# The two FFN down products and the mixer's output product: seven block products in place of eight

## The chip, the cores and the metric

One core of one Trainium2 chip. The metric is the time of one execution on the device, in microseconds (us), as the median of several runs; lower is better.

## What is computed

A decoder trunk on x of 512 tokens by 1024 features: one layer with a short convolution mixer, one with forgetting attention, an FFN behind each. The attention part is not touched by the change. The three products that are changed are `@ w_out` of the mixer and `@ w_down` of the two FFNs:

```python
def short_conv_mixer(xn, w_in, conv_w, w_out):
    proj = xn @ w_in
    b, c, h = jnp.split(proj, 3, axis=-1)
    u = causal_dwconv(c * h, conv_w)
    return (b * u) @ w_out            # 1024 x 1024

def conv_ffn(xn, w_up, conv_w, w_down):
    up = xn @ w_up
    a, g = jnp.split(up, 2, axis=-1)
    a = causal_dwconv(a, conv_w)
    return (jax.nn.silu(a) * g) @ w_down   # 2816 x 1024
...
x = x + short_conv_mixer(rmsnorm(x), ...)
x = x + conv_ffn(rmsnorm(x), ...)
```

## The kernel before

Features lie on the 128 partitions and tokens along the free dimension, so x is eight tiles of 128x512 (k-tiles). Every product is done in fp32r pieces: `split` and `parts` cut an fp32 tile into `hi` (a rounding copy on ACT) and `lo` (source minus hi, on DVE), and `mac` issues hi·hi, hi·lo and lo·hi for each half of 256 tokens: six matmuls of 128x256 for one k-tile and one output tile. Weights come by DMA as 128x1024 tiles (`wraw`, 3 buffers) on SP's queue, and are split 512 columns at a time (`whi`, `wlo`, 4 buffers each), shortly before they are used.

The stages follow each other: the mixer (24 products of eight k-tiles, then the output product `a_out`), FFN0, attention, its output product, FFN1. An FFN makes 22 hidden tiles; tile j needs two up products (`pa`, `pg`) of 48 matmuls each. `pa` is scaled (L316, DVE), convolved (L241 on ACT, L242 and L244 on DVE) and put through silu (L192, ACT); `pg` is scaled (L322, DVE) and multiplied by that on POOL (L323), and the result is split (L162 on ACT, L163 on DVE). When all 22 stand, `project` makes the eight output tiles one after the other, each over 22 k-tiles (132 matmuls), and adds the old x on the way out of PSUM (L271, DVE). `Norm.add` then splits the new x with the next norm's gain (L168, L169) and adds its squares up on POOL (L224).

The order on each engine is what the Tile scheduler makes of the program. PSUM has eight banks of 128x512; `mmps` hands out six of them in turn. One pool `big` of 58 tiles of 128x512 serves all stages.

Of the kernel before, what the change touches and what calls it, by code (L numbers as in the profile page):

```python
# [53 lines left out]
def trunk(ctx: ExitStack, tc: tile.TileContext, x_t, a_in, a_out, up0, down0, wk, wv, wf, wqg, b_out,  # L54
# [40 lines left out]
    x = [G() for _ in range(KT)]  # L95
# [10 lines left out]
    def parts(raw, n):  # L106

        hi = new(wsp, "whi", [P, T], F32R)
        lo = new(wsp, "wlo", [P, T], F32R)
        nc.scalar.copy(out=hi[:, :n], in_=raw)  # L110
        nc.vector.tensor_tensor(out=lo[:, :n], in0=raw, in1=hi[:, :n].bitcast(F32), op=ALU.subtract)  # L111
        return [(hi[:, c:c + P], lo[:, c:c + P]) for c in range(0, n, P)]

    def weights(src, nk=KT):

        cuts = [0, 8] if nk == 8 else [0, 8, 15, 22]
        for c0, c1 in zip(cuts[:-1], cuts[1:]):
            raw = new(wraw, "wraw", [P, 1024], F32)
            nc.sync.dma_start(out=raw[:, :(c1 - c0) * P], in_=src[:, c0 * P:c1 * P])
            for c in range(0, c1 - c0, 4):  # L120
                n = min(4, c1 - c0 - c) * P
                yield from parts(raw[:, c * P:c * P + n], n)
# [18 lines left out]
    def gemm2(srcs, xs, hold=1):

        pss, kept = [], []
        for src in srcs:
            ps = mmps()
            late = []
            for k, w in enumerate(weights(src)):
                if k < KT - hold:
                    mac(ps, w, xs[k], k == 0, False)
                else:  # L150
                    late.append((k, w))
            pss.append(ps)
            kept.append(late)
        for ps, late in zip(pss, kept):
            for k, w in late:
                mac(ps, w, xs[k], False, k == KT - 1)
# [9 lines left out]
    def scaled_split(src, gain):  # L166
        hi, lo = G(F32R), G(F32R)
# [36 lines left out]
    class Norm:  # L204
# [21 lines left out]

        def finish(self):
            ps = bank("at")
            hi, lo = split(self.acc, M(F32R), M(F32R))
# [18 lines left out]
    def back(m):  # L248
        t = new(misc, "ld", [P, T], F32, bufs=3)
        nc.sync.dma_start(out=t, in_=xsp[m])  # L250
        return t

    def project(src, hs, nk, norm, last=False, spilled=False, spill=False, pss=()):

        for m in range(KT):
            if m < len(pss):
                ps = pss[m]
            elif nk == KT and m < 2:
                if m == 0:
                    pss = gemm2((src[0], src[1]), hs)  # L260
                ps = pss[m]
# [68 lines left out]
    def attention(norm, nxt_norm):  # L330
# [426 lines left out]
        for k in range(KT):  # L757
            x[k] = None
# [120 lines left out]
```

## Time and profile before

| | before |
|---|---|
| median of 3 runs | 1234.31 us (1233.61 to 1234.62) |
| the profiled execution | 1233.1 us |
| its span, first to last instruction | 1231.3 us |
| busy: PE / DVE / ACT / POOL | 1216.5 / 678.6 / 537.4 / 203.1 us |
| mean granted TensorE clock | 0.996 of full speed |

The span is the stretch that the trace covers; the profiled execution's own time is 1.8 us longer. Busy times of different engines overlap, so they are to be compared with the span one by one.

### The profile page before, as it was taken

To read this page: it belongs to the slowest core of one execution; us is meant where nothing else is said; L and a number is where in the kernel's file an instruction comes from. 1 tells how busy PE (TensorE), PEld (TensorE's weight loads), DVE (VectorE), ACT (ScalarE), POOL (GpSimd) and SP (SyncE) were. 2 spreads that over 40 slices of the span, in tenths; PEclk is the share of its full clock that TensorE was granted. 3 is DMA by queue.
4 is the path that set the end of the run, shared out by engine and by line. 5 is a ranking of instruction groups with operands and counts; after the bars stand their busy time and mean duration, and the time that the engine had idled before them with its cause. 6 is when DMAs were issued, how large, how long until landed. Compare 5 with 4: busy or idle time off the path is not lost.

```text
span 1231.3 us, 24568 instructions
## 1 busy us (share of the span) xinstructions
PE 1216.5 (99%) x10425; PEld 1189.0 (97%) x10425; DVE 678.6 (55%) x1163; ACT 537.4 (44%) x973; POOL 203.1 (16%) x181
## 2 busy tenths in 40 slices
PE   9999999999999999999999899999999999999998
PEld 8999999999999999999998788889999999999998
DVE  6755556555555533344646787876565555553222
ACT  5433345334333433333556767775543334342221
POOL 0100021111111100000123435442111111110000
PEclk9999999999999999999999999999999999999999
DMA  6233233333333344342342212124233233233341
GB/s 215 87 103 101 88 104 92 97 104 93 97 104 91 93 130 125 121 140 87 95 139 79 84 52 86 53 87 129 86 104 101 89 103 101 89 99 104 116 119 45
DMA packets 39374, 124.14 MB, mean 101 GB/s; under 512 B 4384, under 2 KB 4896, under 8 KB 39264
## 3 DMA queue, kind: packets, MB, share of 16 engines
q1 hardware_dynamic: 38048, 120.41, 31.8%
q10 hardware_dynamic: 1152, 1.97, 0.5%
q8 instruction: 81, 1.33, 0.4%
q14 instruction: 29, 0.24, 0.1%
q0 software_dynamic: 64, 0.20, 0.0%
HBM read 118.33 MB, written 4.23 MB: 100 GB/s over the span
## 4 chain that ended last, share of the span: by engine, by line
PE 90%; ACT 4%; DVE 3%; POOL 2%; issue 1%; DMA 0%; SPq 0%; DVEq 0%; POOLq 0%; ACTq 0%
PE st L131 18%; PE st L130 17%; PE st L132 17%; PE mm L130 11%; PE mm L132 11%; PE mm L131 11%; ACT s L189 1%; PE st L620 1%; PE at L658 1%; PE st L649 1%; POOL m L667 1%; DVE s L624 1%; DVE wlo L111 1%; ACT g L189 1%; ACT g L162 1%
## 5 line engine op out<-in xcount | busy, mean ns | idle before, releaser
L130 PE MATMUL st<-g,whi 128*128 128x256 f32 x1686 | 465.5, 276 | 0.0
L131 PE MATMUL st<-g,whi 128*128 128x256 f32 x1686 | 465.4, 276 | 0.0
L132 PE MATMUL st<-g,wlo 128*128 128x256 f32 x1686 | 465.4, 276 | 0.0
L110 ACT CAST whi<-wraw 128x512 fp32r<-128x512 f32 (+1 forms) x394 | 240.4, 611 | 473.6 <-PE st L131 291.9
L111 DVE TENSOR_TENSOR wlo<-wraw,whi 128x512 fp32r<-128x512 f32 (+1 forms) x394 | 283.6, 720 | 222.9 <-ACT whi L110 218.3
L130 PE MATMUL mm<-g,whi 128*128 128x256 f32 x1242 | 346.2, 279 | 0.0
L131 PE MATMUL mm<-g,whi 128*128 128x256 f32 x1242 | 343.5, 277 | 0.0
L132 PE MATMUL mm<-g,wlo 128*128 128x256 f32 x1242 | 343.5, 277 | 0.0
L130 PEld LDWEIGHTS st<-g,whi 128*128 128x128 f32 x1686 | 316.6, 188 | 0.1
L131 PEld LDWEIGHTS st<-g,whi 128*128 128x128 f32 x1686 | 316.5, 188 | 0.1
L132 PEld LDWEIGHTS st<-g,wlo 128*128 128x128 f32 x1686 | 316.5, 188 | 0.0
L130 PEld LDWEIGHTS mm<-g,whi 128*128 128x128 f32 x1242 | 233.5, 188 | 1.8
L131 PEld LDWEIGHTS mm<-g,whi 128*128 128x128 f32 x1242 | 233.4, 188 | 1.3
L132 PEld LDWEIGHTS mm<-g,wlo 128*128 128x128 f32 x1242 | 233.2, 188 | 0.1
L323 POOL TENSOR_TENSOR m<-m,m 128x512 f32<-128x512 f32 x44 | 69.1, 1573 | 408.3 <-DVE m L322 370.9
L162 ACT CAST g<-m 128x512 fp32r<-128x512 f32 x66 | 40.8, 619 | 90.4 <-POOL m L323 66.8
L163 DVE TENSOR_TENSOR g<-m,g 128x512 fp32r<-128x512 f32 x51 | 36.8, 722 | 67.3 <-ACT g L162 66.7
L224 POOL TENSOR_TENSOR m<-m,m 128x512 f32<-128x512 f32 x21 | 27.9, 1330 | 175.5 <-ACT m L222 153.6
L640 POOL TENSOR_SCALAR s<-s,sm 128x128 f32<-128x128 f32 (+3 forms) x64 | 41.4, 660 | 75.5 <-DVE sm L637 69.2
L189 ACT ACTIVATE s<-s,bb 128x128 f32<-128x128 f32 (+3 forms) x64 | 35.4, 555 | 22.9 <-DVE bb L633 22.8
L241 ACT ACTIVATE m<-m,pr 128x512 f32<-128x512 f32 x52 | 37.7, 725 | 15.9 <-DVE m L316 13.0
L242 DVE SCALAR_TENSOR_TENSOR m<-m,pr,m 128x511 f32<-128x511 f32 x52 | 39.0, 750 | 9.5 <-ACT m L241 9.5
(170 smaller groups left out, 1312.3 us busy)
## 6 DMA issues: line engine op xcount, KB each, us to landing
wraw<-up SPq DMA_DIRECT2D x88, 512.0 KB, 3.5
wraw<-down SPq DMA_DIRECT2D x32, 448.0 KB, 3.5
wraw<-a_in SPq DMA_DIRECT2D x21, 512.0 KB, 3.6
wraw<-down SPq DMA_DIRECT2D x16, 512.0 KB, 3.5
wraw<-wqg SPq DMA_DIRECT2D x16, 512.0 KB, 3.6
wraw<-a_out SPq DMA_DIRECT2D x8, 512.0 KB, 3.5
ld<-xsp SPq DMA_DIRECT2D x16, 256.0 KB, 2.8
wraw<-wv SPq DMA_DIRECT2D x8, 512.0 KB, 3.6
```

Of the source, the lines that this page charges most:

```text
L110: nc.scalar.copy(out=hi[:, :n], in_=raw)
L111: nc.vector.tensor_tensor(out=lo[:, :n], in0=raw, in1=hi[:, :n].bitcast(F32), op=ALU.subtract)
L130: nc.tensor.matmul(ps[:, f], lhsT=lh[0], rhs=rh[0][:, f], start=go, stop=False, skip_group_check=True)
L131: nc.tensor.matmul(ps[:, f], lhsT=lh[0], rhs=rh[1][:, f], start=False, stop=False, skip_group_check=True)
L132: nc.tensor.matmul(ps[:, f], lhsT=lh[1], rhs=rh[0][:, f], start=False, stop=end, skip_group_check=True)
L162: nc.scalar.copy(out=hi, in_=src)
L163: (eng or nc.vector).tensor_tensor(out=lo, in0=src, in1=hi.bitcast(F32), op=ALU.subtract)
L189: chain["exp"] = ordered(nc.scalar.activation(**kw), chain["set"])
L241: nc.scalar.activation(out=y, in_=src, func=AF.Copy, scale=pr[:, col + 2:col + 3])
L242: nc.vector.scalar_tensor_tensor(out=y[:, 1:T], in0=src[:, 0:T - 1], scalar=pr[:, col + 1:col + 2], in1=y[:, 1:T], op0=ALU.mult, op1=ALU.add)
L323: nc.gpsimd.tensor_tensor(out=g, in0=g, in1=y, op=ALU.mult)
L640: nc.gpsimd.tensor_scalar(out=s, in0=s, scalar1=sm[:, e:e + 1], scalar2=1.0, op0=ALU.mult, op1=ALU.mult)
```

## The change

A pair of k-tiles by the two halves of the tokens is a 2x2 arrangement of 128x256 blocks (`f`, a tile of 128x1024), and a pair of output tiles by a pair of k-tiles is a 2x2 arrangement of weight blocks. `Seven` makes the products of such arrangements with seven block products, numbered 1 to 7, in place of eight. For it, `operands` makes the sums and differences of the activation blocks (DVE), and `add_up` those of the weight blocks (POOL: three adds, of 2b, b and b columns, where b is 128 times the number n of pairs of k-tiles in the call). The seven results are put together from two PSUM banks, through copies of a bank on ACT (`early`), sums on DVE and POOL (`sums`, `run`) and `end` on DVE.

The down products are no longer made in one go: `ffn_line` puts a part of them behind hidden tile 6 (n = 3), behind tile 14 (n = 4) and behind tile 21 (n = 4), and x goes through DRAM (`xsp`) between the parts. The last part of each FFN and the mixer's output product are called with `hold`: there the first two `Seven`s run all pairs but the last before the last one is ready. The product of pg and silu on POOL (`late`, L661 after the change) is put into the program one hidden tile later.

Tiles come from pools of each stage. `Line` prepares weights ahead in an order of its own (12 tiles of 128x1024, `w`), in steps that `step`, `mid` and `use` set. `in_order` pins ACT, DVE and POOL to the order of the program in the mixer and in both FFNs. Weights are rearranged on the host so that a `Seven` reads its four blocks side by side.

```diff
-    big = ctx.enter_context(tc.tile_pool(name="big", bufs=58))
-    sp = ctx.enter_context(tc.tile_pool(name="sp", bufs=10))
-    ptp = ctx.enter_context(tc.tile_pool(name="ptp", bufs=6))
     misc = ctx.enter_context(tc.tile_pool(name="misc", bufs=8))
     small = ctx.enter_context(tc.tile_pool(name="small", bufs=3))
-    wraw = ctx.enter_context(tc.tile_pool(name="wraw", bufs=3))
-    wsp = ctx.enter_context(tc.tile_pool(name="wsp", bufs=4))
+    normed_ = ctx.enter_context(tc.tile_pool(name="norm", bufs=16))
+    raws_ = ctx.enter_context(tc.tile_pool(name="raw", bufs=4))
...
+    def in_order(*engines):
...
+    def operands(f, between=None):
+        t, v = S(), blocks(f)
+        tv = blocks(t)
+        nc.vector.tensor_tensor(out=tv[:, 0:2], in0=v[:, 0:4:3], in1=v[:, 1:2].to_broadcast([P, 2, HT]),
+                                op=ALU.subtract)
+        for out, in0, in1 in ((2, tv[:, 1], v[:, 0]), (3, tv[:, 2], v[:, 2])):
+            nc.vector.scalar_tensor_tensor(out=tv[:, out], in0=in0, scalar=-1.0, in1=in1, op0=ALU.mult, op1=ALU.subtract)
+        ops = {}
+        for names, src in (("13", v[:, 0:4:3]), ("57", tv[:, 0:2]), ("64", tv[:, 2:4])):
+            hi, lo = G(F32R), GL(F32R)
+            nc.scalar.copy(out=blocks(hi), in_=src)
+            nc.vector.tensor_tensor(out=blocks(lo), in0=src, in1=blocks(hi).bitcast(F32), op=ALU.subtract)
+            for h, n in enumerate(names):
+                ops[n] = hi[:, h * HT:(h + 1) * HT], lo[:, h * HT:(h + 1) * HT]
+            if between is not None and names == "57":
+                between()
+        g = G(F32R)
+        nc.scalar.copy(out=g[:, 0:HT], in_=v[:, 2])
+        nc.vector.tensor_tensor(out=g[:, HT:T], in0=v[:, 2], in1=g[:, 0:HT].bitcast(F32), op=ALU.subtract)
+        ops["2"] = g[:, 0:HT], g[:, HT:T]
+        return ops
...
+    class Seven:
+        size, raws = 7, 2
+        def __init__(self, src, n):
+            self.n, self.src = n, src
+            self.b = n * P
+        def load(self):
+            b = self.b
+            self.raw = R(), R()
+            for h, r in enumerate(self.raw):
+                nc.sync.dma_start(out=r[:, 0:2 * b], in_=self.src[:, 2 * h * b:2 * (h + 1) * b])
+        done = None
+        def add_up(self):
+            if self.done is None:
+                b, (r0, r1) = self.b, self.raw
+                s, s2 = self.done = S(), S()
+                nc.gpsimd.tensor_tensor(out=blocks(s[:, 0:2 * b], b), in0=blocks(r0[:, 0:2 * b], b),
+                                        in1=blocks(r1[:, b:2 * b], b).to_broadcast([P, 2, b]), op=ALU.add)
+                nc.gpsimd.tensor_tensor(out=s2[:, 0:b], in0=s[:, 0:b], in1=r0[:, b:2 * b], op=ALU.add)
+                nc.gpsimd.tensor_tensor(out=s2[:, b:2 * b], in0=s2[:, 0:b], in1=r1[:, 0:b], op=ALU.add)
+        def prepare(self):
+            self.add_up()
+            b, (r0, r1), (s, s2) = self.b, self.raw, self.done
...
+            for names, raw in (("14", r0), ("75", s), ("63", s2), ("2", r1)):
+                n = len(names) * b
+                hi = W(F32R)
+                lo = hi[:, n:2 * n] if len(names) == 1 else W(F32R)
+                nc.scalar.copy(out=hi[:, 0:n], in_=raw[:, 0:n])
+                nc.vector.tensor_tensor(out=lo[:, 0:n], in0=raw[:, 0:n], in1=hi[:, 0:n].bitcast(F32), op=ALU.subtract)
...
+                if names in ("14", "75"):
+                    yield
+        def go(self, names, xs, ks):
...
+                for p in ks:
+                    c = slice(p * P, (p + 1) * P)
+                    wh, wl = (z[:, c] for z in self.w[m])
+                    xh, xl = xs[p][m]
+                    nc.tensor.matmul(ps, lhsT=wh, rhs=xh, start=m in "17" and p == 0, stop=False, skip_group_check=True)
+                    nc.tensor.matmul(ps, lhsT=wh, rhs=xl, start=False, stop=False, skip_group_check=True)
+                    nc.tensor.matmul(ps, lhsT=wl, rhs=xh, start=False, stop=p == self.n - 1, skip_group_check=True)
...
+        def early(self, names, xs, ks):
+            for m in names:
+                self.go(m, xs, ks)
+                if self.n - 1 in ks and m in "56":
+                    s = M()
+                    nc.scalar.copy(out=s, in_=self.b0 if m == "5" else self.b1)
...
+        def sums(self):
+            nc.vector.tensor_tensor(out=self.v, in0=self.v, in1=self.s, op=ALU.add)
+            nc.gpsimd.tensor_tensor(out=self.v[:, HT:T], in0=self.v[:, 0:HT], in1=self.v[:, HT:T], op=ALU.add)
+        def late(self, names, xs):
+            self.go(names, xs, range(self.n))
...
+        def run(self, xs, norm, last=False, hold=False, old=None):
+            n, sevens = self.n, self.sevens
+            if hold:
+                for sv, names in zip(sevens[:2], ("1576", "157")):
+                    sv.begin()
+                    sv.early(names, xs, range(n - 1))
+                for sv, names in zip(sevens[:2], ("1576", "157")):
+                    sv.early(names, xs, (n - 1,))
+            for q, sv in enumerate(sevens):
+                if hold and q < 2:
+                    if q == 1:
+                        sv.line.use_next(sv)
+                        self.store(0, norm, last, (0,))
+                        sv.early("6", xs, range(n))
+                        self.store(0, norm, last, (1,))
+                else:
+                    if q == 0:
+                        sv.line.use(sv)
+                    sv.begin()
+                    sv.early("15", xs, range(n))
+                    sv.line.use_next(sv)
+                    if q:
+                        self.store(q - 1, norm, last, (0,))
+                    sv.early("76", xs, range(n))
+                    if sv.line.pending:
+                        sv.line.step()
+                    if q:
+                        self.store(q - 1, norm, last, (1,))
+                olds = [back(m, old) for m in (2 * q, 2 * q + 1)]
+                sv.sums()
+                nc.gpsimd.tensor_tensor(out=olds[0][:, HT:T], in0=olds[0][:, HT:T], in1=sv.v[:, 0:HT], op=ALU.add)
+                sv.line.mid()
+                sv.late("234", xs)
+                self.end(q, sv, last, olds)
+            self.store(q, norm, last)
+        def end(self, q, sv, last, old):
...
+            nc.vector.tensor_tensor(out=x[m1], in0=o1, in1=sv.v, op=ALU.subtract)
+            nc.vector.tensor_tensor(out=x[m1][:, l], in0=x[m1][:, l], in1=sv.b1[:, r], op=ALU.subtract)
+            if last:
+                nc.scalar.dma_start(out=out_t[m1], in_=x[m1])
+            if last and q == KT // 2 - 1:
+                for f, eng in ((r, nc.scalar), (l, nc.sync)):
+                    nc.vector.tensor_tensor(out=x[m0][:, f], in0=sv.b0[:, f], in1=o0[:, f], op=ALU.add)
+                    eng.dma_start(out=out_t[m0][:, f], in_=x[m0][:, f])
+            else:
+                nc.vector.tensor_tensor(out=x[m0], in0=sv.b0, in1=o0, op=ALU.add)
...
+    def ffn_line(line, up, down):
+        seq, k0 = [], 0
+        for j in range(JT):
+            seq.append(("up", j, [line.add(One(up[j, c])) for c in range(2)]))
+            if j in (6, 14, JT - 1):
+                n = (j + 1) // 2 - k0
+                seq.append(("down", j, Project(line, [z[:, 4 * k0 * P:4 * (k0 + n) * P] for z in down], n)))
+                k0 += n
+        return seq
...
+            def late(g=g, y=y, j=j, f=f):
+                end = j == JT - 1
+                (nc.vector if end else nc.gpsimd).tensor_tensor(out=half(f, j), in0=g, in1=y, op=ALU.mult)
+                if j % 2:
+                    us.append(operands(f, part.sevens[0].line.step if end else None))
```

PE has 10461 rows in the program before and 10149 in the changed one.

The first place is **POOL in FFN0**, from hidden tile 2 to tile 6. Before, where a row is the product of the scaled pg and silu of one hidden tile:

```order
L323 TENSOR_TENSOR m_2685<-m_2685,m_2621 128x512
L323 TENSOR_TENSOR m_2817<-m_2817,m_2753 128x512
L323 TENSOR_TENSOR m_2949<-m_2949,m_2885 128x512
L323 TENSOR_TENSOR m_3081<-m_3081,m_3017 128x512
L323 TENSOR_TENSOR m_3213<-m_3213,m_3149 128x512
```

Now, from tile 4 into the first part of the down product (n = 3), where L661 is that product, L406 to L409 the adds of weight blocks of one `Seven`, and L458 and L538 the adds that put its results together:

```order
L661 TENSOR_TENSOR sum_2963<-m_2961,m_2907 128x512
L661 TENSOR_TENSOR sum_2963<-m_3070,m_3016 128x512
L406 TENSOR_TENSOR sum_3096<-raw_2852,raw_2853 128x768
L408 TENSOR_TENSOR sum_3097<-sum_3096,raw_2852 128x384
L409 TENSOR_TENSOR sum_3097<-sum_3097,raw_2853 128x384
L458 TENSOR_TENSOR m_3252<-m_3252 128x256
L538 TENSOR_TENSOR ld_3278<-ld_3278,m_3252 128x256
L406 TENSOR_TENSOR sum_3346<-raw_3101,raw_3102 128x768
L408 TENSOR_TENSOR sum_3347<-sum_3346,raw_3101 128x384
L409 TENSOR_TENSOR sum_3347<-sum_3347,raw_3102 128x384
```

Between two products there was nothing; each `Seven` has now put five adds there.

The second place is **DVE at the end of hidden tile 5** (`pg` of tile 5 at L322 before and L655 now). Before, with L111 the weight splits of the up products, L163 the `lo` of tile 5, and L316, L242 and L244 the scaling and convolution of tile 6:

```order
L322 TENSOR_TENSOR m_3081<-st_3022,r_2405 128x512
L111 TENSOR_TENSOR wlo_3186<-wraw_3155,whi_3185 128x512
L163 TENSOR_TENSOR g_3085<-m_3081,g_3084 128x512
L111 TENSOR_TENSOR wlo_3224<-wraw_3221,whi_3223 128x512
L316 TENSOR_TENSOR m_3147<-st_3088,r_2405 128x512
L111 TENSOR_TENSOR wlo_3252<-wraw_3221,whi_3251 128x512
L242 SCALAR_TENSOR_TENSOR m_3149<-m_3147,pr,m_3149 128x511
L244 SCALAR_TENSOR_TENSOR m_3149<-m_3147,pr,m_3149 128x510
```

Now, where L365 to L380 are `operands` of tiles 4 and 5, L420 the weight splits of the part's first `Seven`, and L649 the scaled `pa` of tile 6:

```order
L655 TENSOR_TENSOR m_3070<-st_3021,r_2426 128x512
L365 TENSOR_TENSOR sum_3073<-sum_2963 128x512
L368 SCALAR_TENSOR_TENSOR sum_3073<-sum_3073,sum_2963 128x256 x2
L373 TENSOR_TENSOR gl_3078<-sum_2963,g_3077 128x512
L373 TENSOR_TENSOR gl_3082<-sum_3073,g_3081 128x512
L373 TENSOR_TENSOR gl_3086<-sum_3073,g_3085 128x512
L380 TENSOR_TENSOR g_3089<-sum_2963,g_3089 128x256
L420 TENSOR_TENSOR w_3093<-raw_2708,w_3092 128x768
L420 TENSOR_TENSOR w_3106<-sum_2847,w_3105 128x768
L420 TENSOR_TENSOR w_3110<-sum_2848,w_3109 128x768
L420 TENSOR_TENSOR w_3113<-raw_2709,w_3113 128x384
L649 TENSOR_TENSOR m_3165<-st_3116,r_2426 128x512
```

Ahead of the scaling of tile 6 stood three splits; now eleven rows stand there, of which the last four are the weight splits of a `Seven`.

The third place is **ACT there**, from the convolution of tile 6 on. Before, with L241 and L192 the convolution's first step and silu, L110 weight casts and L162 the cast of a hidden tile:

```order
L241 ACTIVATE m_3149<-m_3147,pr 128x512
L110 CAST whi_3289<-wraw_3287 128x512
L192 ACTIVATE m_3149<-m_3149 128x512
L110 CAST whi_3317<-wraw_3287 128x512
L162 CAST g_3216<-m_3213 128x512
L110 CAST whi_3355<-wraw_3353 128x512
L110 CAST whi_3383<-wraw_3353 128x512
```

Now, with L466 and L304 in their place, L419 weight casts, and L449 the copies of the two banks of the first `Seven`:

```order
L419 CAST w_3113<-raw_2709 128x384
L466 ACTIVATE m_3167<-m_3165,pr 128x512
L304 ACTIVATE m_3167<-m_3167 128x512
L419 CAST w_3224<-raw_2852 128x768
L449 COPY m_3252<-st_3232 128x512
L449 COPY m_3272<-mm_3233 128x512
L419 CAST w_3274<-sum_3096 128x768
```

The copies that the first `Seven`'s last products wait for have come in behind silu of tile 6 and one weight cast of the second `Seven`.

## Rows read from the trace of the kernel before

**Rows 1.** The page: span, and busy time of each engine.

```profile
span 1231.3 us, 24568 instructions
...
PE 1216.5 (99%) x10425; PEld 1189.0 (97%) x10425; DVE 678.6 (55%) x1163; ACT 537.4 (44%) x973; POOL 203.1 (16%) x181
```

**Rows 2.** Busy time by stretch: mixer to FFN0, and attention output (columns in its first row).

```profile
core 0: us, PE busy (x) PEld busy (x) DVE busy (x) ACT busy (x) POOL busy (x), PEclk, DMA share, GB/s
...
30.00:360.00 330.00, 330.00 (x2909) 329.82 (x2908) 189.96 (x271) 129.23 (x209) 43.81 (x31) 1.00 0.31 97
...
820.00:900.00 80.00, 79.92 (x688) 78.58 (x687) 51.88 (x80) 42.98 (x75) 18.71 (x17) 1.00 0.35 109
```

**Rows 3.** Timeline of DVE, down product of FFN1: start, duration, idle before it in brackets.

```profile
1122.90 0.69 DVE L271 TENSOR_TENSOR g<-st,g 128x512 f32<-128x512 f32 x1 [0.81 <-PE st L132]
1123.51 0.55 DVE L111 TENSOR_TENSOR wlo<-wraw,whi 128x384 fp32r<-128x384 f32 x1
1126.21 0.69 DVE L111 TENSOR_TENSOR wlo<-wraw,whi 128x512 fp32r<-128x512 f32 x1 [2.15 <-ACT whi L110]
...
1137.86 0.69 DVE L271 TENSOR_TENSOR g<-st,g 128x512 f32<-128x512 f32 x1 [0.81 <-PE st L132]
```

**Rows 4.** Timeline of PE, the same place.

```profile
1122.70 0.28 PE L130 MATMUL st<-s,whi 128*128 128x256 f32 x1
1122.82 0.28 PE L131 MATMUL st<-s,whi 128*128 128x256 f32 x1
1122.93 0.28 PE L132 MATMUL st<-s,wlo 128*128 128x256 f32 x1
```

**Rows 5.** Groups of ACT by shape: busy us and mean ns, then idle before.

```profile
L110 ACT CAST whi<-wraw 128x512 fp32r<-128x512 f32 x362 | 224.0, 620 | 418.8 <-PE st L131 254.8 <-PE mm L131 134.3 <-ACT m L222 10.6
...
L110 ACT CAST whi<-wraw 128x384 fp32r<-128x384 f32 x32 | 16.4, 514 | 54.8 <-PE st L131 37.1 <-PE mm L131 17.7
...
L500 ACT COPY g<-mm 128x512 f32<-128x512 f32 x16 | 9.2, 577 | 1.0 <-PE mm L132 1.0
```

**Rows 6.** Groups of POOL by shape.

```profile
L323 POOL TENSOR_TENSOR m<-m,m 128x512 f32<-128x512 f32 x44 | 69.1, 1573 | 408.3 <-DVE m L322 370.9 <-ACT m L192 37.4
L224 POOL TENSOR_TENSOR m<-m,m 128x512 f32<-128x512 f32 x21 | 27.9, 1330 | 175.5 <-ACT m L222 153.6 <-issue 21.9
...
L640 POOL TENSOR_SCALAR s<-s,sm 128x512 f32<-128x512 f32 x16 | 15.6, 989 | 18.4 <-DVE sm L637 18.4
...
L640 POOL TENSOR_SCALAR s<-s,sm 128x128 f32<-128x128 f32 x16 | 5.8, 377 | 13.2 <-DVE sm L637 11.8 <-DVE mx L632 1.4
```

**Rows 7.** Timeline of POOL, attention output product with the norm of FFN1.

```profile
844.12 1.35 POOL L224 TENSOR_TENSOR m<-m,m 128x512 f32<-128x512 f32 x1 [7.40 <-ACT m L222]
846.33 1.52 POOL L224 TENSOR_TENSOR m<-m,m 128x512 f32<-128x512 f32 x1 [0.86 <-ACT m L222]
```

**Rows 8.** Timeline of DVE, the same place.

```profile
844.22 0.68 DVE L271 TENSOR_TENSOR g<-st,ld 128x512 f32<-128x512 f32 x1
844.82 1.19 DVE L111 TENSOR_TENSOR wlo<-wraw,whi 128x512 fp32r<-128x512 f32 x1
...
846.60 0.68 DVE L271 TENSOR_TENSOR g<-mm,ld 128x512 f32<-128x512 f32 x1
847.20 1.19 DVE L111 TENSOR_TENSOR wlo<-wraw,whi 128x512 fp32r<-128x512 f32 x1
```

**Rows 9.** Timeline of DVE, hidden tile 21 of FFN1.

```profile
1102.50 0.69 DVE L316 TENSOR_TENSOR m<-mm,r 128x512 f32<-128x512 f32 x1 [1.02 <-PE mm L132]
```

**Rows 10.** Timeline of ACT, the same place.

```profile
1105.68 0.63 ACT L192 ACTIVATE m<-m 128x512 f32<-128x512 f32 x1
```

**Rows 11.** DMA issues: KB each, us from issue to landing.

```profile
wraw<-down SPq DMA_DIRECT2D x16, 512.0 KB, 3.5
...
ld<-xsp SPq DMA_DIRECT2D x16, 256.0 KB, 2.8
```

**Rows 12.** Timeline of DVE, its last row.

```profile
1227.62 0.76 DVE L271 TENSOR_TENSOR g<-st,g 128x256 f32<-128x256 f32 x2 [8.47 <-PE st L132]
```

More of the change, by code (lines that the diff above doesn't have):

```diff
@@ L94, in trunk @@
     cs = const.tile([P, C_ET], F32, tag="cs", name="cs")
-    x = [G() for _ in range(KT)]
+    pools = stage(("g", 16), ("sum", 4), ("gl", 16), ("w", 12))
+    x = [GL() for _ in range(KT)]
     ones = const.tile([P, P], F32R, tag="ones", name="ones")
@@ L106, in parts, with weights @@
     def parts(raw, n):
[L108 to L122, printed above, removed]
+        step = 2 * T if "w" in pool else T
+        for c0 in range(0, n, step):
+            c1 = min(n, c0 + step)
+            if step > T:
+                hi, lo = W(F32R), W(F32R)
+            else:
+                hi, lo = new(pool["whi"], "whi", [P, T], F32R), new(pool["wlo"], "wlo", [P, T], F32R)
+            w = c1 - c0
+            nc.scalar.copy(out=hi[:, :w], in_=raw[:, c0:c1])
+            nc.vector.tensor_tensor(out=lo[:, :w], in0=raw[:, c0:c1], in1=hi[:, :w].bitcast(F32), op=ALU.subtract)
+            yield from ((hi[:, c:c + P], lo[:, c:c + P]) for c in range(0, w, P))
+    def weights(src):
+        raw = R()
+        nc.sync.dma_start(out=raw, in_=src)
+        yield from parts(raw, D)
     def mac(ps, lh, rh, first, last):
@@ L136, in gemm, with __init__ @@
+    class One:
+        size, raws = 2, 1
+        def __init__(self, src):
+            self.src = src
+        def load(self):
+            self.raw = R()
+            nc.sync.dma_start(out=self.raw, in_=self.src)
+        def prepare(self):
+            self.w = list(parts(self.raw, D))
+            yield
+    def gemm(unit, xs, hold=0):
+        if unit.at >= unit.line.ready or not hold:
+            unit.line.use(unit)
+        unit.line.mid(hold)
         ps = mmps()
-        for k, w in enumerate(weights(src, nk)):
-            mac(ps, w, xs[k], k == 0, k == nk - 1)
@@ L139, in gemm @@
-        return ps
[L141 to L156, printed above, removed]
+        for k, w in enumerate(unit.w):
+            mac(ps, w, xs[k], k == 0, k == KT - 1)
@@ L157, in gemm2 @@
+        return ps
+    def gemm2(units, xs, hold=1, between=None):
+        for unit in units:
+            unit.line.use(unit)
+            unit.line.mid()
+            if between is not None:
+                between()
+                between = None
+        pss = [mmps() for _ in units]
+        for ks in (range(KT - hold), range(KT - hold, KT)):
+            for unit, ps in zip(units, pss):
+                for k in ks:
+                    mac(ps, unit.w[k], xs[k], k == 0, k == KT - 1)
         return pss
@@ L257, in project @@
                 ps = pss[m]
[L258 to L261, printed above, removed]
[L262 to L273 removed]
+            else:
+                ps = gemm(src[m], hs)
@@ L281, in mixer, with half @@
+    def half(f, k):
+        return f[:, (k % 2) * T:(k % 2 + 1) * T]
+    def mixer(line, norm, nxt, first):
+        tiles_ = {}
+        for i, c in [(1, 0), (1, 1), (1, 2)] + [(i, c) for i in range(2, KT) for c in range(3)]:
+            tiles_[i, c] = line.add(One(a_in[i, c]))
+        out = Project(line, a_out, KT // 2)
+        seq = ffn_line(line, up0, down0)
         bu = []
         for i in range(KT):
-            ph, pc, pb = early.pop(i, (None, None, None))
-            if ph is None:
-                ph = gemm(a_in[i, 0], norm.xs)
+            ph, pc, pb = first if i == 0 else (None, None, None)
+            if i == 1:
+                ph = early
+            elif i:
+                ph = gemm(tiles_[i, 0], norm.xs)
@@ L756, in attention @@
         kept.append(ps2)
-        for k in range(KT):
-            x[k] = None
-        project(b_out, og, KT, nxt_norm, spilled=True, pss=kept)
+        line = Line(8, 2)
+        project([line.add(One(z)) if m >= len(kept) else None for m, z in enumerate(b_out)], og, nxt_norm, kept)
     use_exp_ln()
```

276 lines of the change are left out of this document (206 added, 70 removed).

## The prediction

> **What bounds the kernel now.** I read the page first: PE is busy for 1216.5 of the 1231.3 us of the span, DVE for 678.6, ACT for 537.4, POOL for 203.1 [rows 1]. The reader should see that only PE is full over the whole, so fewer matmuls can pay; that says nothing yet of a single stretch. So next the busy times by stretch: from the mixer to FFN0's middle PE is busy for all of 330 us, with DVE at 190, POOL at 44, the TensorE clock at 1.00 and the DMA engines at 0.31; in the attention output product with its norm, 79.92 of 80 [rows 2]. There PE waits for nothing, and each matmul taken away is worth its pitch. That comes from the evictions in the down product of FFN1, 14.96 us apart for 132 matmuls, which is 0.1133 us each [rows 3]; starts of neighbours, 0.11 to 0.12 apart, agree [rows 4]. Last I looked where DVE and POOL work at the same time, since the change gives both more to do [rows 7, 8].
>
> **What it removes.** In a pair of output tiles by a pair of k-tiles, 24 matmuls become 21, of the same shape. The mixer's output product has 384 and loses 48; each down product has 1056 and loses 132; together 312, which is also the difference of PE's row counts, 10461 less 10149. 312 x 0.1133 is 35.4 us off PE. Each matmul had its own weight load before (as many PEld as PE [rows 1]) and has it still, so I keep the pitch.
>
> **What it adds, where it is hidden.** Prices first. DVE with two inputs in SBUF takes 0.69 for 512 columns and 0.55 for 384 [rows 3]; on that line 768 are 0.97, 1024 are 1.25, 256 are 0.41. ACT casts at 0.62 and 0.51 give 0.83 and 1.05 for 768 and 1024; a copy of a bank takes 0.58 [rows 5]. POOL's add of 512 columns takes 1.33 [rows 6]; for other widths the trace has no add, so I bound it by the slope of POOL's other operation (989 less 377 ns over 384 columns, 1.59 ns each [rows 6]) and by proportion: 1024 columns 2.14 to 2.66, 768 columns 1.74 to 2.00, 384 columns 1.00 to 1.13, 256 columns 0.67 to 0.92. I take the middles: 2.4, 1.87, 1.07, 0.8. The adds of weight blocks then cost 5.06 us of POOL for a `Seven` with n = 4 and 4.01 with n = 3, against PE's 84 x 0.1133 = 9.52 and 63 x 0.1133 = 7.14. By itself POOL keeps up. So does ACT (about 4.9 us a `Seven` at n = 4 with its two copies). The extra rounds of x through DRAM are 256 KB a tile, landing in 2.8 us [rows 11], on DMA engines that are a third busy, and the weights come two `Seven`s ahead at 3.5 us [rows 11]; I cost them at nothing. If that cover were gone, one landing for each part, 3 us, would be the price. In attention only the pools change on PE's side; nothing. At the end, two halves of 0.76 in all follow the last matmul [rows 12]; now one subtraction of 256 columns stands ahead: +0.4.
>
> **Where DVE and POOL meet.** DVE's 512-column split takes 1.19 in place of 0.69 where it starts inside a POOL add, and ends 0.54 after that add's end (846.01 against 845.47); the one from 847.20 goes the same way; an eviction from PSUM that starts inside the second add takes its usual 0.68 [rows 7, 8]. So two-input work on DVE waits until POOL's instruction is over, and its net time is then its own less 0.15: 1.10 for 1024 columns, 0.82 for 768, 0.40 for 384. The Trainium skill (SBUF — State Buffer, "Who interferes with whom") states this as a rule: a DVE instruction with two SBUF inputs and a GpSimd instruction that reads SBUF share a port pair, and whoever issues second is blocked for the whole instruction. The trace agrees, with 1.19 for 0.69. If each of the waits below were for a whole add, as that rule allows, the entry terms would be at their upper ends and the sum 1223.
>
> **The entries of the parts.** What is late next is found at the start of each part, where ACT and DVE are in pinned order. Take n = 4, with time 0 at the last matmul of hidden tile 13. Scaling 0.7, POOL's product 1.33, then `operands`: 0.69 + 2 x 0.41 + 3 x 0.69 before the sixth block can be released, some 6 us with hand-offs. From there POOL has the second `Seven`'s adds, 5.06 (they need the tile that `operands` frees), and DVE 0.4 of `operands` and the four splits of the first `Seven`, 3 x 1.10 + 0.54 = 3.84. They take turns, so DVE is through at 15.3, or at 14.1 if POOL's last add comes last. Only then follows the scaling of tile 14, which PE had ready at 5.4, and up to the end of silu that takes 3.81 (1102.50 to 1106.31 [rows 9, 10]); then a cast of 1.05 and the copy of the first bank, 0.58: 19.5 to 20.7. PE needs that copy when it comes to block product 2: two up products (96 matmuls, 10.88) and 48 more (5.44) after 0, at 16.3. It stalls 3.2 to 4.4 us. With n = 3: 12.2 + 3.81 + 0.83 + 0.58 = 17.4 against 10.88 + 4.08 = 14.96, 2.4 to 3.5. Without the turns on the port both come out at zero (15.9 against 16.3; 14.8 against 14.96). I take the lower ends, as DVE's queue has no gap there and should win turns: 2 x 3.2 + 2 x 2.4 = 11.2 for the four middle parts.
>
> In the last parts, PE reaches block product 5 of the second `Seven` 45 matmuls, 5.1 us, after the last up product. Its weight split stands on DVE behind scaling, product, 0.69 + 0.82, and two splits of `operands`: 5.5 with itself, 5.8 with hand-offs, so 0.7 late with no port and 0.7 + 5.06 if all of POOL's adds fall there. Between the ends I take 3.1 for each FFN; for the mixer, where fewer adds are left over, half, 1.6. Sum 7.8.
>
> **The sum.** 1233.1 (profiled execution; its span of 1231.3 and 1.8 around it) - 35.4 + 0.4 + 11.2 + 7.8 = 1217.1. The median of the runs is 1.2 above that execution, so 1218.3: **1218**.
>
> **Rivals.** *The whole gain*: the entries hide, because turns on the port fall better than I count or the order leaves slack: 1234.3 - 35.4 + 0.4 = 1199. For it: without the port my own timelines fit, by 0.1 to 0.4 us; against it: that is thin, and [rows 7, 8].
>
> *Port-bound, not faster*: the parts that also feed a norm (mixer's output, last part of FFN0) have eight square adds on POOL (1.33 each) and eight two-input gain splits on DVE (0.6 net) besides. POOL there: 3 x 5.06 (the first `Seven`'s adds lie ahead) + 4 x 1.6 + 10.6 = 32.2. DVE's two-input work: 3 x 3.84 + 8 x 0.54 + 8 x 0.6 = 20.6. Together 52.8 on one port, in 4 x 9.52 = 38.1 of PE: 14.7 over, 29 in two such parts. Against it: the end of that work can slide under the next up products, as in [rows 2] PE loses 0.08 of 80 us with the same norm beside it, but with a third of the weight adds' load. A part with n = 4 and no norm comes to 37.4 of 38.1, so nothing lost is won back; n = 3 to 31.3 of 28.6. All paid, less the entry terms it contains (4.7), gives 1243; it decides from 16 us on, where the gain is gone.
>
> *The change doesn't do what it says*: the pitch is not kept, with products that go back and forth between half banks and have narrow `rhs` blocks of other tiles: at 0.117 on the remaining matmuls, 10149 x 0.0037 = 37 us, no change, 1234. Nothing in [rows 4] speaks for it.
>
> **Chances.** The forecast (1208 to 1230) 0.45; the whole gain 0.25; the port-bound case (1230 to 1248) 0.25; no change in PE's time 0.05. About 0.2% (2.5 us) is what a measurement of this kernel can tell from no change. So faster 0.45 + 0.25 + 0.02 = 0.72, within it 0.06 + 0.03 = 0.09, slower 0.19. The range from 1197 to 1239 takes in the whole gain and the port-bound case with some four fifths of its price paid; the forecast alone would have 1208 to 1230.
>
> **What would show it.** PE's busy time down by about 35 and its idle time up by about 19, in seven places: releaser ACT `m` L449 (the bank copies) at the four middle parts, 2 to 4 us each, and DVE `w` L420 at the last parts. POOL's adds at L406 of 2.1 to 2.7 (n = 4); DVE L420 at over 1.5 where it meets them, and 1.25 alone. If PE's waits in the parts sum to less than 8, the whole gain is right; if PE waits for L420 or POOL's sums through the norm parts by over 8 us each, the port-bound case is. I would be wrong altogether if the up stages, which I left alone, lost time, or if a bank or a pool's tile came free too late in attention.

## The result and the profile after

The changed kernel takes 1301.86 us (median; 1300.64 to 1303.64) against 1234.31 before: 1.0549 times as long, 95% interval 1.0531 to 1.0568. I had forecast 1218 with a range of 1197 to 1239. Its page, span and busy times (compare [rows 1]):

```profile
span 1299.8 us, 24419 instructions
...
PE 1253.4 (96%) x10113; PEld 1220.2 (94%) x10113; DVE 921.2 (71%) x1274; ACT 593.5 (46%) x972; POOL 431.3 (33%) x319
```

There are 312 matmuls fewer, and PE is busy for 37 us more. That alone says that a matmul has become dearer. PE idles 46.4 us in place of 14.8, as the forecast had it in kind, but more. The page's TensorE clock tells a third thing: its mean is 0.988, before 0.996.

Where PE is full, the number of matmuls in 20 us shows the first. The same stretch of FFN1's up products by windows, before and after (the number behind PE's busy time is that of its matmuls, the last three columns are the clock, the DMA share and GB/s):

```profile
940.00:960.00 20.00, 20.00 (x179) 20.00 (x178) 11.39 (x17) 7.91 (x13) 3.19 (x2) 1.00 0.32 106
```

```profile
940.00:960.00 20.00, 20.00 (x169) 20.00 (x168) 13.41 (x20) 8.65 (x12) 1.31 (x2) 1.00 0.25 79
```

179 against 169, at full clock and with PE waiting for nothing, in a stage whose matmuls the change doesn't touch. Matmul for matmul, on PE's timeline after:

```profile
944.73 0.28 PE L160 MATMUL st<-n,w 128*128 128x256 f32 x1
944.85 0.28 PE L161 MATMUL st<-n,w 128*128 128x256 f32 x1
944.97 0.28 PE L162 MATMUL st<-n,w 128*128 128x256 f32 x1
945.09 0.28 PE L160 MATMUL st<-n,w 128*128 128x256 f32 x1
```

They start 0.12 apart. This step from one matmul's start to the next is its pitch. Over all matmuls with 256 columns whose next neighbour starts less than 0.125 us later, the mean pitch is 113.55 ns before (9768 steps) and 119.60 ns after (9286).

The second, PE's idle time, is in its waits (engine, what it waited for, us in all, times, longest):

```profile
PE st L436 <- ACT m L449: 10.9, 7, 2.2
PE mm L436 <- ACT m L449: 8.0, 5, 2.2
...
PE st L438 <- DVE w L420: 2.8, 5, 0.9
PE mm L438 <- DVE w L420: 2.5, 3, 1.2
PE st L160 <- ACT n L268: 2.4, 1, 2.4
```

L449 is the copy of a bank and L420 a weight split of a `Seven`: the two releasers that the prediction named. And one entry, that of the part behind hidden tile 14, as the prediction drew it. POOL, DVE and ACT there:

```profile
398.60 2.52 POOL L406 TENSOR_TENSOR sum<-raw,raw 128x1024 f32<-128x1024 f32 x1 [3.53 <-DVE gl L373]
401.20 2.15 POOL L408 TENSOR_TENSOR sum<-sum,raw 128x512 f32<-128x512 f32 x1
403.43 2.15 POOL L409 TENSOR_TENSOR sum<-sum,raw 128x512 f32<-128x512 f32 x1
```

```profile
398.77 3.43 DVE L420 TENSOR_TENSOR w<-raw,w 128x1024 fp32r<-128x1024 f32 x1
402.13 4.54 DVE L420 TENSOR_TENSOR w<-sum,w 128x1024 fp32r<-128x1024 f32 x2
406.59 0.68 DVE L420 TENSOR_TENSOR w<-raw,w 128x512 fp32r<-128x512 f32 x1
407.19 0.68 DVE L649 TENSOR_TENSOR m<-st,r 128x512 f32<-128x512 f32 x1
```

```profile
410.30 0.63 ACT L304 ACTIVATE m<-m 128x512 f32<-128x512 f32 x1 [1.67 <-DVE m L469]
410.83 1.03 ACT L419 CAST w<-raw 128x1024 fp32r<-128x1024 f32 x1
411.77 0.58 ACT L449 COPY m<-st 128x512 f32<-128x512 f32 x1
```

POOL's first add and DVE's first split start within 0.17 us. The split ends 1.08 after the add, taking 3.43 for the 1.25 it takes alone; the next two take 4.54 together for 2.5. Only then is tile 14 scaled (407.19), and the bank copy comes behind silu and the cast. PE waited 2.4 us there. None of these four DVE rows has idle time in front of it: DVE did not wait for a sum of POOL's here, it stood still inside its own instructions.

The windows over a part show the third, the clock:

```profile
160.00:180.00 20.00, 16.32 (x132) 15.71 (x131) 19.18 (x16) 8.38 (x13) 16.11 (x9) 1.00 0.47 158
180.00:200.00 20.00, 16.79 (x132) 16.04 (x132) 18.66 (x17) 9.26 (x15) 12.32 (x9) 1.00 0.58 188
200.00:220.00 20.00, 19.07 (x143) 18.78 (x144) 14.18 (x15) 11.32 (x15) 2.89 (x2) 0.91 0.51 181
```

In the mixer's output product PE is idle 6.9 of 40 us, DVE is busy for 38 of them, and in the window behind it the mean granted clock is 0.91: a piece of it ran at 1.2 in place of 2.4 GHz. Within the span the trace has 30.7 us at the lower level, 10.2 before; half of the difference, 10.2, is lost.

So the 68.5 us by which the span grew come to: 312 matmuls, -35.4; pitch on the 9286 steps, 6.05 ns each, +56.2; gaps of 0.26 us and more, 48.2 us in 39 against 8.5 in 11, less 28 pitches that they contain, +36.3; clock, +10.2; together +67.3.

### The profile page after: what moved, and what is told of

Same layout as the page of the kernel before. It is cut to its first block, busy times and chain, and to the rows that moved or that the text cites. A ratio compares the mean times of both kernels' runs of the same rounds, so it can differ in the third digit from the quotient of the medians.

```text
span 1299.8 us, 24419 instructions
## 1 busy us (share of the span) xinstructions
PE 1253.4 (96%) x10113; PEld 1220.2 (94%) x10113; DVE 921.2 (71%) x1274; ACT 593.5 (46%) x972; POOL 431.3 (33%) x319
## 4 chain that ended last, share of the span: by engine, by line
PE 70%; DVE 14%; ACT 6%; issue 5%; POOL 4%; DMA 1%; SPq 0%; DVEq 0%; ACTq 0%; POOLq 0%
PE st L162 11%; PE st L161 11%; PE st L160 11%; PE mm L160 8%; PE mm L162 8%; PE mm L161 8%; DVE w L420 5%; PE st L438 2%; PE st L436 2%; PE st L437 2%; DVE gl L551 2%; ACT s L301 1%; PE mm L438 1%; PE mm L436 1%; PE mm L437 1%
## 5 line engine op out<-in xcount | busy, mean ns | idle before, releaser
L160 PE MATMUL st<-n,w 128*128 128x256 f32 x1216 | 345.5, 284 | 3.6 <-ACT n L268 2.4
L162 PE MATMUL st<-n,w 128*128 128x256 f32 x1216 | 345.6, 284 | 0.8 <-DVE w L145 0.8
L161 PE MATMUL st<-n,w 128*128 128x256 f32 x1216 | 345.6, 284 | 0.4 <-DVE n L269 0.4
L160 PEld LDWEIGHTS st<-n,w 128*128 128x128 f32 x1216 | 234.8, 193 | 4.1 <-ACT n L268 2.6
L162 PEld LDWEIGHTS st<-n,w 128*128 128x128 f32 x1216 | 234.9, 193 | 1.0 <-DVE w L145 1.0
L161 PEld LDWEIGHTS st<-n,w 128*128 128x128 f32 x1216 | 234.7, 193 | 0.7 <-DVE n L269 0.6
L661 POOL TENSOR_TENSOR sum<-m,m 128x512 f32<-128x512 f32 x42 | 64.5, 1536 | 349.9 <-DVE m L655 282.1
L145 DVE TENSOR_TENSOR w<-raw,w 128x1024 fp32r<-128x1024 f32 x109 | 133.2, 1241 | 56.4 <-ACT w L144 56.3
L162 PE MATMUL mm<-n,w 128*128 128x256 f32 x528 | 149.4, 283 | 0.0
L161 PE MATMUL mm<-n,w 128*128 128x256 f32 x528 | 149.4, 283 | 0.0
L160 PE MATMUL mm<-n,w 128*128 128x256 f32 x528 | 149.4, 283 | 0.0
L436 PE MATMUL st<-g,w 128*128 128x256 f32 x460 | 133.1, 289 | 12.5 <-ACT m L449 10.9
L438 PE MATMUL st<-g,w 128*128 128x256 f32 x460 | 132.9, 289 | 2.9 <-DVE w L420 2.8
L144 ACT CAST w<-raw 128x1024 fp32r<-128x1024 f32 x109 | 111.2, 1044 | 49.4 <-DMA raw<-up 22.0
L466 ACT ACTIVATE m<-m,pr 128x512 f32<-128x512 f32 x52 | 37.6, 724 | 181.9 <-DVE m L649 143.4
L437 PE MATMUL st<-gl,w 128*128 128x256 f32 x393 | 112.2, 286 | 0.0
L436 PEld LDWEIGHTS st<-g,w 128*128 128x128 f32 x460 | 90.6, 197 | 14.1 <-ACT m L449 12.3
L160 PEld LDWEIGHTS mm<-n,w 128*128 128x128 f32 x528 | 101.4, 192 | 0.0
L161 PEld LDWEIGHTS mm<-n,w 128*128 128x128 f32 x528 | 101.4, 192 | 0.0
L162 PEld LDWEIGHTS mm<-n,w 128*128 128x128 f32 x528 | 101.4, 192 | 0.0
L420 DVE TENSOR_TENSOR w<-raw,w 128x1024 fp32r<-128x1024 f32 (+3 forms) x56 | 85.2, 1525 | 13.6 <-ACT w L419 13.4
```

The costliest lines, as they stand in the source:

```text
L144: nc.scalar.copy(out=hi[:, :w], in_=raw[:, c0:c1])
L145: nc.vector.tensor_tensor(out=lo[:, :w], in0=raw[:, c0:c1], in1=hi[:, :w].bitcast(F32), op=ALU.subtract)
L160: nc.tensor.matmul(ps[:, f], lhsT=lh[0], rhs=rh[0][:, f], start=go, stop=False, skip_group_check=True)
L161: nc.tensor.matmul(ps[:, f], lhsT=lh[0], rhs=rh[1][:, f], start=False, stop=False, skip_group_check=True)
L162: nc.tensor.matmul(ps[:, f], lhsT=lh[1], rhs=rh[0][:, f], start=False, stop=end, skip_group_check=True)
L420: nc.vector.tensor_tensor(out=lo[:, 0:n], in0=raw[:, 0:n], in1=hi[:, 0:n].bitcast(F32), op=ALU.subtract)
```

## The experiments

**Theory A** for the pitch: it depends on where the two operands of a matmul lie in SBUF. In the program before, the moving operands (`big`) start at 384 modulo 512 bytes, and the weights (`whi`, `wlo`) at 448, because the pool `small`, with 576 bytes, lies between them. In the changed program `small` lies ahead of both, and both start at 448. **Rival B**: the wide weight tiles, the pinned order or the new work on other engines. **Theory P** for the waits: POOL's adds and DVE's splits take turns on one port. **Rival O**: the pinned order alone; **rival D**: DVE's load, whoever adds.

`e1_gap` puts unused pieces between the pools, so that the offsets are 384 and 448 again:

```diff
     small = ctx.enter_context(tc.tile_pool(name="small", bufs=3))
+    ctx.enter_context(tc.tile_pool(name="gap0", bufs=1)).tile([P, 112], F32, tag="gap0", name="gap0")
...
-    pools = stage(("g", 16), ("sum", 4), ("gl", 16), ("w", 12))
+    pools = stage(("g", 16), ("sum", 4), ("gl", 16), ("gap1", 16), ("w", 12))
...
```

The same is done for the pools of attention and FFN1, in lines left out here.

> The changed kernel with three unused pieces of SBUF (448, 64 and 448 bytes a partition) between its pools, so that the moving operands of nearly all matmuls start at 384 modulo 512 bytes and their weights at 448, as before the change; nothing else is changed. Theory A (the pitch of a matmul depends on where its two operands lie: 119.6 ns with both at 448, 113.5 ns with 384 and 448): some 9490 matmuls get 6.1 ns back, 58 us, and it runs at about 1244 us. Rival B (the longer pitch comes from weight tiles of 1024 columns, pinned order or more DMA and POOL work): it stays at 1302 us with 169 matmuls in 20 us of an up stage.

1279.03 us, 1.0368 times the kernel before (1.0313 to 1.0423). Faster by 23, not by 58. Most neighbours are 113 or 114 ns apart again, but some stretches keep to 118; the waits for the bank copies (L449, here L453) grew from 18.9 to 25.4, and PE waits 9.1 us at the start of attention: the pieces had moved weight tiles there over others that are freed later, and SP's third pair of weight loads came 24 us behind the second, in place of 12.

`e2_before_same` turns it round, in the kernel before:

```diff
+    ctx.enter_context(tc.tile_pool(name="gap0", bufs=1)).tile([P, 112], F32, tag="gap0", name="gap0")
     wraw = ctx.enter_context(tc.tile_pool(name="wraw", bufs=3))
```

> The kernel before with one unused piece of 448 bytes ahead of its weight pools, so that weights start at 384 modulo 512 bytes, as the moving operands do. Theory A: about 9200 matmuls take 119.6 in place of 113.5 ns, 56 us more, about 1290 us. Rival B: 1234 us as before.

1290.20 us, 1.0449 (1.0421 to 1.0478), with no other change in the program. Its windows:

```profile
940.00:960.00 20.00, 20.00 (x169) 20.00 (x169) 11.13 (x17) 7.26 (x12) 3.18 (x2) 1.00 0.28 81
```

448 unused bytes cost 57 us (the kernel before took 1233.23 beside it), where theory A had 56. This kernel has no wide weight tiles, no pins and no new work on other engines, so rival B falls.

`m1_map` leaves out the whole computation and has matmuls with their weight loads alone, one pair of offsets after the other without a pause.

> Only matmuls of 128x256 in fp32r, 48 at each of 25 pairs of offsets (moving operand, weights) from a multiple of 512 bytes plus 64; it leaves out the reference's whole computation. Theory A: two or three pitches, 113 to 114 ns where the weights lie 64 bytes behind the moving operand (first and last pair), 118 to 120 where both have the same offset. Rival B: one pitch for all pairs.

Three of its stretches on PE's timeline (start, time of the group, and how many). First pair (64 bytes apart), second pair (same offset), and the first pair again at the end:

```profile
11.39 5.46 PE L41 MATMUL ps<-mv,w 128*128 128x256 f32 x45
```

```profile
16.93 5.44 PE L41 MATMUL ps<-mv,w 128*128 128x256 f32 x44
```

```profile
147.83 5.38 PE L41 MATMUL ps<-mv,w 128*128 128x256 f32 x46
```

Less the 0.28 of the last one, and by the number less one: 117.7, 120.0 and 113.3 ns. Over all 25 pairs, the means are 119.8 to 120.0 where both offsets are the same modulo 256 (seven pairs), and 117.4 to 118.7 for the others, but for two at 113.3, whose offsets are 64 bytes apart. Five more that are 64 bytes apart gave 117.8 or 117.9, so theory A holds for equal offsets and not as it stood for 64. The pair that gave 117.7 first gave 113.3 last. So an unequal offset doesn't fix the pitch: equal ones exclude the short one here, and at 64 bytes apart a stretch falls into 113 or 118.

`e3_no_adds`, against theory P:

```diff
-                s, s2 = self.done = S(), S()
-                nc.gpsimd.tensor_tensor(out=blocks(s[:, 0:2 * b], b), ...
-                nc.gpsimd.tensor_tensor(out=s2[:, 0:b], ...
-                nc.gpsimd.tensor_tensor(out=s2[:, b:2 * b], ...
+                self.done = r0, r1
```

> The kernel of e1_gap without the three POOL adds of weight blocks in each Seven (the weight splits read the raw tiles in their place, so the sums of weight blocks are left out). Theory P (the stalls at the parts come from these adds and DVE's two-input splits taking turns on one port): some 20 to 30 of the 32 us of added PE waits go, and the half-speed clock behind them; about 1210 to 1220 us if e1_gap takes 1244. Rival O (they come from the pinned orders of ACT and DVE, whatever POOL does): at most 8 us less than e1_gap.

1224.93 us, 0.9934 (0.9912 to 0.9955): 54 less than e1_gap, more than the waits and the clock that I had put on it, and still with the 9.1 us wait at attention. Its trace is of the longest of its ten executions, 1235.76. PE's wait for L449 is down to this:

```profile
PE st L436 <- ACT m L449: 1.9, 2, 1.0
```

The orders are as pinned as before, so rival O falls as the whole cause. From 190 to 507 us this execution lay at the 118 ns pitch.

`e1b_gap` has the weight tiles of attention lie exactly over tiles that end early:

```diff
-    pools = stage(("g", 16), ("sum", 4), ("gl", 16), ("gap1", 16), ("w", 12))
+    pools = stage(("g", 16), ("gap1", 16), ("sum", 4), ("gap2", 112), ("gl", 16), ("gap3", 16), ("w", 12))
```

> As e1_gap, with two more unused pieces, so that the weight tiles of attention lie exactly over tiles that end early, as in the changed kernel, and the order of loads at the start of attention is that of the changed kernel again. Both theories on the waits: the 9.1 us wait there goes, with some 5 us of half clock behind it; 1279 less 14, about 1265 us, give or take 10 for the pitch (113 or 118 ns) that a stretch falls into. If it stays at 1279, the wait had another cause than the layout.

1268.93 us, 1.0280 (1.0240 to 1.0319); the 9.1 us wait is gone, and the third pair of loads comes 12 us behind the second again. This is the changed kernel with the pitch mended. PE is busy for 1204.1 us, 49 less than in the changed kernel; gaps are 64.2 us, 16 more. What the pitch gave back was partly taken by waits, since the work that PE waits for has not become shorter.

`e4_adds_dve` moves the 84 adds of weight blocks to DVE; `e4_adds_mixed` moves only the 42 that are not made ahead, during an up product. The edit of the first:

```diff
-                nc.gpsimd.tensor_tensor(out=blocks(s[:, 0:2 * b], b), ...
+                nc.vector.tensor_tensor(out=blocks(s[:, 0:2 * b], b), ...
...
-                self.units[k].add_up()
```

> The kernel of e1b_gap with all three adds of weight blocks of each Seven on DVE, next to the split that needs them, and none ahead of its turn. Theory P (the adds cost PE time because POOL and DVE take turns on one port and POOL is slow): an n = 4 Seven then has 1.25 + 2 x 0.69 = 2.6 us of adds in place of POOL's 6.2; at least 20 us faster than e1b_gap, 1225 to 1245 us. Rival D (DVE is the bound whoever adds): no faster than e1b_gap.

> As e4_adds_dve, but the adds of the Seven that follows an up product stay on POOL, early, as in the changed kernel; the others are on DVE. Theory P: between e1b_gap and e4_adds_dve at the entries of the parts, better than both only if POOL finds DVE idle there.

1246.06 us (1.0093; 1.0063 to 1.0122), 23 less than e1b_gap, and 1257.24 (1.0188; 1.0167 to 1.0208), between the two, with nothing won by the early adds on POOL. DVE's groups at L420 of e1b_gap and of this kernel (lines are L424 and L423 there), us busy and mean ns:

```profile
L424 DVE TENSOR_TENSOR w<-sum,w 128x1024 fp32r<-128x1024 f32 x40 | 63.6, 1606 | 10.4 <-ACT w L423 10.4
```

```profile
L423 DVE TENSOR_TENSOR w<-sum,w 128x1024 fp32r<-128x1024 f32 x40 | 51.2, 1296 | 2.9 <-ACT w L422 2.9
```

DVE does 84 adds more and is busy for less (907.5 against 918.6 us): it had been standing still inside its own instructions. Rival D falls as the whole cause; what the adds cost on DVE itself is in the table below.

`e5_free_order` takes the pins away from e1b_gap, `e7_dve_free` from e4_adds_dve:

```diff
-    with tc.issue_after(...), in_order(*pinned):
+    with tc.issue_after(...), ExitStack():
...
-        with in_order(*pinned):
+        with ExitStack():
```

> The kernel of e1b_gap without the pinned order of ACT, DVE and POOL from the mixer to FFN0 and in FFN1: the scheduler orders them. If the stalls come from what the pins put ahead of the bank copies, PE's waits for L453 shrink by more than half and it is 15 us or more faster than e1b_gap. If the port is the cause whatever the order, it is within 8 us of it.

> The kernel of e4_adds_dve without the pinned order of ACT, DVE and POOL. If the pins cost time of their own, as in e5_free_order, 8 to 13 us less than e4_adds_dve, about 1235; if the pins only hurt while POOL holds the port, as e4_adds_dve or slower.

1256.17 us (1.0176; 1.0152 to 1.0200), 12.8 less, between the two outcomes that I had named, and 1235.13 (1.0009; 0.9986 to 1.0032), 10.9 less. In e5_free_order PE waits for L453, the bank copies, for 29.5 us, no less than with the pins (25.6): the pins cost time, but not in these waits.

`e8_all_dve` moves the two adds of 256 columns as well, `e9_all_free` drops the pins on top:

```diff
-            nc.gpsimd.tensor_tensor(out=self.v[:, HT:T], ...
+            nc.vector.tensor_tensor(out=self.v[:, HT:T], ...
...
-                nc.gpsimd.tensor_tensor(out=olds[0][:, HT:T], ...
+                nc.vector.tensor_tensor(out=olds[0][:, HT:T], ...
```

> The kernel of e4_adds_dve with the two adds of 256 columns that put the seven results together (1.22 and 1.08 us on POOL) on DVE as well, 0.41 each. Theory P: POOL holds the port for 2.3 us less in each Seven and DVE works 0.8 more; 28 Sevens, a part of each on PE's path: 8 to 16 us less than e4_adds_dve, 1230 to 1238. Rival D (DVE's own load is the bound by now): no faster.

> The kernel of e8_all_dve without the pinned order. The sum of both expectations, 1222 to 1230, if they are independent; it would then be faster than the kernel before.

1248.09 us (1.0128; 1.0095 to 1.0160), no faster than e4_adds_dve; but its trace has 3448 neighbours at 116 to 119 ns, that of e4_adds_dve 1038, some 11 us, while PE's gaps in the parts are 5.4 us shorter (table below). So the two adds did take waits away, and the pitch took the time back. They were also worth less than expected: 1.22 and 1.08 are means with POOL's own waiting in them, and alone such an add takes 0.74. e9_all_free takes 1220.92 us, 0.9901 (0.9871 to 0.9930): **1% faster than the kernel before.** Its page:

```profile
span 1218.6 us, 24397 instructions
...
PE 1191.7 (98%) x10113; PEld 1160.6 (95%) x10113; DVE 911.4 (75%) x1414; ACT 598.0 (49%) x972; POOL 214.3 (18%) x179
```

POOL is back at its load of before, and PE waits for the bank copies for 5.9 us.

`e10_no_gap` is that kernel without the unused pieces.

> The kernel of e9_all_free without the unused pieces of SBUF, so that moving operands and weights start at the same offset (448) modulo 512 bytes again, as in the changed kernel. With the pitch at 119.6 ns in place of a mean near 114.3 on some 9500 matmuls, 50 us more, less a few that PE then no longer waits: 1262 to 1272 us. If the offset is worth only the 33 us by which e1b_gap was faster than the changed kernel, 1254.

1264.36 us, 1.0247 (1.0221 to 1.0274): 43.4 more, in the expected interval and beyond what the pieces gave in e1b_gap. Where PE waits for less, the pitch is worth more.

PE's gaps in the seven parts (steps of 0.26 us and more up to each matmul of a part, less one pitch each), from the traced execution of each kernel, in us:

| kernel | gaps in the parts |
|---|---|
| changed kernel | 31.3 |
| e1_gap: pitch mended | 40.4 |
| e3_no_adds: that, without the weight adds | 3.9 |
| e1b_gap: pitch mended, loads as in the changed kernel | 41.8 |
| e5_free_order: e1b_gap without pins | 33.4 |
| e4_adds_mixed: e1b_gap, half of the adds on DVE | 34.8 |
| e4_adds_dve: all weight adds on DVE | 26.1 |
| e7_dve_free: that, without pins | 19.7 |
| e8_all_dve: e4_adds_dve, 256-column adds on DVE too | 20.7 |
| e9_all_free: that, without pins | 9.4 |
| e10_no_gap: that, at the long pitch | 3.1 |

Without the adds the waits are nearly gone. With the adds on DVE instead of POOL, in the same pinned order, 15.7 of 41.8 us go and 26.1 stay. So the turns with a slower POOL are shown as one cause of these waits, and not as the whole: the adds' own time on DVE in a pinned order is another, and e9_all_free needed both steps. How much of the 15.7 is the turns and how much POOL's slower adds is not separated by these runs.

## Why the prediction was wrong

**The step that failed** is "Each matmul had its own weight load before (as many PEld as PE) and has it still, so I keep the pitch." I took the shape for the whole price, and never asked what the new pools do to addresses. The pitch went from 113.55 to 119.60 ns, and the up stages, which the change leaves alone, lost time with the rest (169 matmuls for 179 in 20 us): the sign that the prediction itself gave for being wrong altogether. The trace of before held the warning. In its first 25 us, where weights and moving operands come out of the same pool (`g` both), PE's timeline reads:

```profile
17.74 0.28 PE L130 MATMUL st<-g,g 128*128 128x256 f32 x1
17.86 0.28 PE L131 MATMUL st<-g,g 128*128 128x256 f32 x1
17.98 0.28 PE L132 MATMUL st<-g,g 128*128 128x256 f32 x1
18.10 0.28 PE L130 MATMUL st<-g,g 128*128 128x256 f32 x1
```

0.12 apart, against 0.1133 in [rows 3, 4]. The rival in which the pitch is not kept had the wrong reason (half banks and narrow blocks in the parts), 0.117, and a chance of 0.05; measured are 119.6 ns, in the up products as much as in the parts. That term alone, 56.2 us, carries the time from the forecast to 1274.

**The saving** was as counted: 312 matmuls, and e3_no_adds, without POOL's weight adds, is faster than before although it waits 9.1 us at attention.

**The entries of the middle parts** were right in their mechanism: gaps of 2.2 and 2.4 us in FFN0, 2.2 and 2.7 in FFN1, 9.5 together against 11.2, with the releaser, the order of events and the split over twice its time as drawn. e3_no_adds has none of these gaps, as the prediction had it for no turns on the port. That the size came out so near is in part luck, for the longer pitch brings PE later to the copy that it needs. At the pitch that I had kept, in e1b_gap, the same four are 4.0, 3.3, 3.5 and 3.3 us, 14.2 together, between the sums of my lower and upper ends (11.2 and 15.8). PE's waits for the bank copies over the whole of e1b_gap, against 10.9 and 8.0 in the changed kernel:

```profile
PE st L440 <- ACT m L453: 14.6, 7, 3.5
PE mm L440 <- ACT m L453: 11.0, 5, 3.2
```

**The last parts** were mis-sized. Their gaps come to 6.0 us in the mixer's output product, 9.2 in FFN0 and 6.7 in FFN1, 21.9 against my 7.8 (all less one pitch each); another 3.5 at FFN0's start and 2.5 at FFN1's I had not seen at all, and those stay without the weight adds (3.8 and 2.3 in e3_no_adds). The rival *port-bound* had the cause in part, 14.7 us over in each part with a norm; I gave it 0.25 and set its price beside the forecast in place of half of it inside. Its prices for POOL were those of an add alone, and so they held: 0.74 for 256 columns where I took 0.8, and 2.40 as the shortest of 1024 columns where I took 2.4. Missing was that POOL's adds, too, get longer where DVE works beside them: of 28 adds at L458, the ten with no DVE instruction beside them took 0.74 in the mean. POOL's rows before and in the mixer's output product:

```profile
128.15 2.41 POOL L406 TENSOR_TENSOR sum<-raw,raw 128x1024 f32<-128x1024 f32 x1
...
157.46 0.75 POOL L458 TENSOR_TENSOR m<-m 128x256 f32<-128x256 f32 x1 [9.81 <-DVE m L457]
...
158.85 3.39 POOL L406 TENSOR_TENSOR sum<-raw,raw 128x1024 f32<-128x1024 f32 x1
...
170.56 1.65 POOL L458 TENSOR_TENSOR m<-m 128x256 f32<-128x256 f32 x1 [0.63 <-DVE m L457]
```

Over the kernel the means are 1.22 and 1.08 for 256 columns (28 each; L458, L538) and 2.82 for 1024.

**The clock** had no term at all. Of nine stretches of 3.4 us at the lower level two are in attention, where the kernel before has both of its own (10.2 us together), and seven begin where PE has just waited, in the parts or at a stage's start. [rows 2] show only stretches at 1.00; the ones in attention, next to them, would have shown the price. With all these terms, 56.2 for the pitch, 14.1 more in the last parts, 1.7 less in the middle ones, 6.0 at the two FFNs' starts and 10.2 of clock, the forecast becomes 1303, against 1302 measured.

## What to carry to other kernels

A change of pools is a change of addresses: before costing a matmul by its shape, compare its pitch (start to start) in stretches of the trace that take operands from other pools, and look at where the new pools put weights and moving operands. A second engine that shares a port is no free engine: add up both engines' two-input work for each part, and put the whole overrun into the sum, not into a rival. And waits grow when the thing that hid them gets faster: e1b_gap got 49 us of PE time back and kept 33.

## What I had not expected of the hardware

The pitch of a matmul of 128x256 in fp32r takes one of about three values, 113.3, 117.7 and 120.0 ns, by the offsets of its two operands (the same modulo 256 bytes: 120) and, at unequal offsets, by something that can change and then stays (e3_no_adds kept to 118 from 190 to 507 us). What picks 113 or 118 was not found; the spread of e1_gap's runs, 1273 to 1287 us, is of that size, though no run shows that this is its cause. The Trainium skill (SBUF — State Buffer, "Who interferes with whom") gives TensorE two read ports, for the moving operand and for the weights, and calls them independent. m1_map, where the pitch goes by how the two offsets stand to each other, and e2_before_same, 4.5% longer by an unused piece alone, don't agree with that, and the measurement decides; that the two reads hinder each other is argued from this, not shown. The same section's rule for DVE and GpSimd agrees with the rows above: 3.43 us for a split of 1.25.
